# A decode beside a prompt: held time put aside and repaid at a quarter of the running time

## The chip, the core and the metric

The kernel runs on one core of one Trainium2 chip. The metric is the device time of one execution in microseconds. The core has five engines, each with its own queue of instructions that it executes in order: TensorE (PE, matrix products), VectorE (DVE), ScalarE (ACT), GpSimd (POOL) and SyncE (SP, which here only starts transfers). Engines wait for each other by semaphores.

## The reference, cut to what matters

One inference step of a decoder layer for two groups of rows that share the weights: a prompt of 1024 rows, and eight sequences that each add one row ("sample") and attend to 8192 cached rows in pages.

```python
def step(x):                                   # for the prompt and for the sample
    h = rmsnorm(x, g_mix) @ w_in               # q, k, v, forget logit, u, z
    att = fox_attend(q, k, v, cumsum(logf))    # sample: k, v, logf from the paged cache
    sgu = u * (causal_chunk(w_s) @ z + b_s)
    x = x + concat(rmsnorm(att), rmsnorm(sgu)) @ w_o
    x = x + cross_attend(rmsnorm(x), mk, mv, w_cq, w_co)   # 4 heads, 256 memory rows
    x = x + conv_ffn(rmsnorm(x), w_up, conv_w, w_down)     # D_FF = 2816, width 3
    return rmsnorm(x, g_final)

def fox_sample(q, k, v, logf, k_pool, v_pool, logf_pool, page_table):
    k_all = concat(k_pool[page_table], k)
    v_all = concat(v_pool[page_table], v)
    c = cumsum(concat(logf_pool[page_table], logf))
    return fox_attend(q, k_all, v_all, c)      # softmax(q.k / 8 + c_q - c_k) . v
```

All in float32, D_MODEL 1024, 8 attention heads of 64. The outputs also hold the prompt's keys and values, the memory's keys and values (`o_mk`, `o_mv`) and the states for a next step.

## The kernel before

**Arithmetic.** A float32 product is made of three products of rounded parts: `split` writes the high part on ACT (L235, with a scale L238) and the rest on DVE (L236, with a scale L239); `gemm3` (L272 to L274) multiplies high by high, high by low and low by high. Weights come by `wraw` (L249, a 512 KB load that SP starts into one of four buffers `wr`) and are split into `wh` and `wl`.

**The prompt's work** is a Python generator, `prompt()`, which goes through the phases `p1`, `att0`, `attx`, `att1`, and then, for each half of 512 rows, `mid` and `ffn`: `mid0`, `ffn0`, `mid1`, `ffn1`. A `mid` phase is the output projection (`out_proj`, whose products are L1055 to L1057), the norm and transposition (`norm_T`: transposes L1106, splits L239), and cross-attention (`cross`, projections by w_cq and w_co at L1073 to L1075 and in `out_proj`). In cross-attention, for each of four heads: `fetch` loads the head's `o_mk` and `o_mv` (SP, L1126 and L1128); `keys` transposes the keys (PE L1153) and copies them (ACT L1157); `weigh` multiplies queries and keys (PE L1170), takes maxima (DVE L1172), exponentials (ACT L1175, L1178), the reciprocal of the sums (DVE L1181) and scales (ACT L1183); `turned` transposes the weights (PE L1190, copied by ACT L1191); `gather` multiplies by the values (PE L1198) and splits the result, the low part on DVE (L236, `u`). PSUM banks named `ba` and `bb` are used in turn; a bank is free for the next product when the engine that reads it has done so. Each time it has recorded a piece of work, the generator yields `t`, an estimate in microseconds of the TensorE time just recorded.

**The decode** is a second generator, `sample()`: for each sequence 16 K steps and 16 V steps over its cached rows, then `sample_rest()` for the remaining layers of the eight rows. A K step (`kstep`, L1404) fetches 1 MB of keys by an indirect DMA that POOL starts (L1407) into one of four buffers `kv`, multiplies by the query on DVE (L1423) and reduces on DVE (L1427): two multiplies and two reductions in the `mid` phases or while held, one of each of twice the size otherwise. A V step (`vstep`) fetches 1 MB of values (L1469) into the same four buffers and multiplies on PE (L1475, into `dv`; two V steps go to PE together, 16 matmul records in the profile).

**What sets the order.** A loop at the end of `build` takes the prompt's yields one by one. `acc` collects the yielded time; whenever it reaches the pace of the phase (`PACE`, for instance 8.0 us per decode step in `mid0`, 8.5 in `ffn0`, 6.8 in `mid1`, 2.5 in `ffn1`, and 2.9 once the decode has come to its rest), one step of the decode is recorded and the pace taken off. `most` limits how many steps one yield may let through: the whole number of paces in `t`, plus one. `held[0]` stops the decode altogether for a while: `out_proj` sets it after its last group of two row tiles (L1083), `ffn` sets it in its last down-projection when the merge of the second half runs beside it (L1325), and `norm_T` (L1116) and the end of a feed-forward stage (L1888) release it. While it is held, `acc` goes on collecting.

The recorded program then goes through a planner, which re-orders the instructions of each engine by its own costs and due times; DVE and PE instructions of the decode are tied to what was recorded just before them (`behind`, with `last`), so that a step that is recorded later is also planned later.

The lines of the loop that count here:

```python
        acc[0] += t
        most = int(t / PACE[phase[1] or phase[0]]) + 1
        while bgs and not held[0] and most and acc[0] >= PACE[phase[1] or phase[0]]:
            most -= 1
            acc[0] -= PACE[phase[1] or phase[0]]
            w = next(bgs[0], None)
```

Of the kernel before, what the change touches and what calls it, by code (L numbers as in the profile page):

```python
# [78 lines left out]
def build(nc, tc, ctx, a, phases=None):  # L79
# [918 lines left out]
    held = [False]  # L998
# [347 lines left out]
    bgs, acc, phase = [], [0.0], ["p1", None]  # L1346
# [545 lines left out]
    def sample():  # L1892
        yield from decode()
        phase[1] = "rest"
        yield from sample_rest()


    bgs.append(sample())
    seen = 0
    for t in prompt():  # L1900
        ins = nc.cur_bb.bb.instructions
        for e in (ENG.DVE, ENG.PE):
            for i in range(len(ins) - 1, max(seen, len(ins) - 400) - 1, -1):
                if ins[i].engine == e:
                    last[e] = ins[i]
                    break
        if paused[0]:
            t = 0.0
        acc[0] += t
        most = int(t / PACE[phase[1] or phase[0]]) + 1  # L1910
        while bgs and not held[0] and most and acc[0] >= PACE[phase[1] or phase[0]]:
            most -= 1
            acc[0] -= PACE[phase[1] or phase[0]]
            w = next(bgs[0], None)
            if w is None:
                bgs.pop()
            else:
                acc[0] -= (w - 1) * PACE[phase[1] or phase[0]]
        seen = len(nc.cur_bb.bb.instructions)
# [92 lines left out]
```

## Time and profile before

| | us |
|---|---|
| median of 3 runs | 1816.22 (1815.31 to 1817.39) |
| profiled execution | 1820.56 |
| its span | 1818.4 |
| PE busy | 1745.0 (96%) |
| DVE busy | 1397.5 (77%) |
| ACT busy | 734.4 (40%) |
| POOL busy | 510.0 (28%) |

The profile is of one execution, so its own time stands beside its span: 2.16 us lie around the span, and this execution took 4.34 us more than the median. In the rows of the profile, `L1170` is a line of the kernel, `out<-in` names the tiles that an instruction writes and reads, `x8` says how many instructions are grouped, and a bracket such as `[4.19 <-DVE u L236]` gives the idle time of the engine just before them and what ended it. The names of the weights' transfers carry the tile (`wr<-w_co`), those of the decode carry the cache (`kv<-cache_k`). The phases `mid0` to `ffn1` lie at about 560 to 720, 720 to 1110, 1110 to 1360, and from 1360 us to the end of the span.

### The profile page before, as it was taken

How to read it: one execution, taken by the hardware profiler on the slowest of the kernel's cores; microseconds unless marked ns; L12 is line 12 of the kernel's file. 1: busy time of each engine (PE TensorE's matmuls, PEld its weight loads, DVE VectorE, ACT ScalarE, POOL GpSimd, SP SyncE). 2: the span in 40 equal slices, each digit the busy share in tenths (PEclk: the TensorE clock that was granted, in tenths of full speed). 3: DMA queues.
4: the chain of work that ended last, by engine and by line, in shares of the span. 5: the costliest groups of instructions: out<-in, count | busy, mean ns of one | idle time of the engine just before them, and what ended most of it. 6: DMA issues, size and time to landing. Idle time of an engine off the chain costs nothing.

```text
span 1818.4 us, 25090 instructions
## 1 busy us (share of the span) xinstructions
PE 1745.0 (96%) x9637; PEld 1294.9 (71%) x9637; DVE 1397.5 (77%) x1729; ACT 734.4 (40%) x1378; POOL 510.0 (28%) x461
## 2 busy tenths in 40 slices
PE   8999999888998999999999999989899999999997
PEld 5887776656676767777777776766576778767775
DVE  4689668888788877999989899898875549845344
ACT  6332365455643544433333244235353324332332
POOL 1252334332133432223332333334222111011110
PEclk9999999899999999999999999989999999999999
DMA  8886889777696986679878779988787777568982
GB/s 295 306 297 231 302 297 329 242 266 224 219 398 257 342 310 260 257 285 340 316 279 311 271 306 340 381 300 324 290 309 290 267 268 265 179 266 289 359 314 82
DMA packets 157074, 521.06 MB, mean 287 GB/s; under 512 B 20874, under 2 KB 40842, under 8 KB 124186
## 3 DMA queue, kind: packets, MB, share of 16 engines
q0 software_dynamic: 57168, 341.14, 49.5%
q1 hardware_dynamic: 92874, 165.73, 26.4%
q10 hardware_dynamic: 6912, 12.59, 1.8%
q8 instruction: 76, 1.25, 0.3%
q14 instruction: 44, 0.36, 0.1%
HBM read 495.47 MB, written 23.93 MB: 286 GB/s over the span
## 4 chain that ended last, share of the span: by engine, by line
PE 72%; DMA 10%; issue 7%; DVE 6%; ACT 2%; POOL 2%; SPq 0%; POOLq 0%; DVEq 0%; ACTq 0%
PE ba L272 11%; PE ba L274 11%; PE ba L273 11%; PE bb L272 5%; PE bb L273 5%; PE bb L274 5%; PE dv L1475 5%; DMA kv<-cache_k,io 3%; DMA wr<-w_in 2%; DMA kv<-cache_v,io 1%; PE dv L321 1%; PE dv L1751 1%; PE ba L1056 1%; PE ba L1055 1%; PE ba L1057 1%
## 5 line engine op out<-in xcount | busy, mean ns | idle before, releaser
L235 ACT ACTIVATE wh<-wr 128x1024 fp32r<-128x1024 f32 (+2 forms) x220 | 228.9, 1044 | 489.2 <-PE ba L273 156.0
L236 DVE TENSOR_TENSOR wl<-wr,wh 128x1024 fp32r<-128x1024 f32 (+2 forms) x220 | 262.5, 1200 | 175.6 <-PE ba L274 65.7
L1407 POOL DMA_INDIRECT kv<-cache_k,io x128 | 205.6, 1606 | 551.2 <-DVE s L1427 318.9
L1423 DVE TENSOR_TENSOR kv<-kv,d 128x1024 f32<-128x1024 f32 (+1 forms) x156 | 258.0, 1681 | 35.1 <-DMA kv<-cache_k,io 35.1
L1427 DVE TENSOR_REDUCE s<-kv 128x16 f32<-128x1024 f32 (+1 forms) x156 | 258.2, 1674 | 0.1
L1469 POOL DMA_INDIRECT kv<-cache_v,io x128 | 165.3, 1291 | 282.8 <-PE dv L1475 191.8
L272 PE MATMUL ba<-u,wh 128*128 128x512 f32 (+1 forms) x560 | 220.3, 395 | 1.7 <-ACT u L238 1.7
L273 PE MATMUL ba<-u,wh 128*128 128x512 f32 (+1 forms) x560 | 220.2, 393 | 1.7 <-DVE u L239 1.5
L274 PE MATMUL ba<-u,wl 128*128 128x512 f32 (+1 forms) x560 | 219.5, 393 | 0.0
L272 PE MATMUL ba<-wh,u 128*128 128x512 f32 (+1 forms) x495 | 186.9, 379 | 0.9 <-ACT u L235 0.9
L273 PE MATMUL ba<-wl,u 128*128 128x512 f32 (+1 forms) x495 | 185.4, 375 | 1.2 <-DVE wl L236 1.2
L274 PE MATMUL ba<-wh,u 128*128 128x512 f32 (+1 forms) x495 | 183.8, 376 | 0.0
L272 PEld LDWEIGHTS ba<-u,wh 128*128 128x128 f32 x560 | 106.8, 191 | 30.6 <-issue 5.6
L273 PE MATMUL bb<-u,wh 128*128 128x512 f32 (+1 forms) x304 | 119.4, 393 | 9.2 <-DVE u L239 9.2
L274 PEld LDWEIGHTS ba<-u,wl 128*128 128x128 f32 x560 | 106.9, 191 | 29.1 <-issue 6.1
L273 PEld LDWEIGHTS ba<-u,wh 128*128 128x128 f32 x560 | 106.7, 191 | 27.5 <-issue 2.7
L1475 PE MATMUL dv<-kv,s 128*32 128x512 f32 x1024 | 124.2, 598 | 1.8 <-DMA kv<-cache_v,io 1.8
L272 PE MATMUL bb<-u,wh 128*128 128x512 f32 (+1 forms) x304 | 119.4, 393 | 0.0
L274 PE MATMUL bb<-u,wl 128*128 128x512 f32 (+1 forms) x304 | 118.6, 390 | 0.0
L272 PEld LDWEIGHTS ba<-wh,u 128*128 128x128 f32 x495 | 93.0, 188 | 26.0 <-issue 6.9
L274 PEld LDWEIGHTS ba<-wh,u 128*128 128x128 f32 x495 | 92.8, 188 | 21.5 <-issue 3.7
L273 PEld LDWEIGHTS ba<-wl,u 128*128 128x128 f32 x495 | 93.1, 188 | 19.7 <-DVE wl L236 1.9
(425 smaller groups left out, 3255.9 us busy)
## 6 DMA issues: line engine op xcount, KB each, us to landing
wr<-w_up SPq DMA_DIRECT2D x88, 512.0 KB
kv<-w_up POOLq DMA_DIRECT2D x22, 1024.0 KB, 8.0
wr<-w_down SPq DMA_DIRECT2D x40, 512.0 KB
kv<-w_down POOLq DMA_DIRECT2D x11, 1024.0 KB, 8.5
wr<-w_in SPq DMA_DIRECT2D x16, 512.0 KB
wr<-w_o SPq DMA_DIRECT2D x16, 512.0 KB
wr<-w_cq SPq DMA_DIRECT2D x16, 512.0 KB
wr<-w_co SPq DMA_DIRECT2D x16, 512.0 KB
```

The lines of the kernel that those rows point to most:

```text
L235: nc.scalar.activation(h, src, AF.Copy)
L236: nc.vector.tensor_tensor(l, src, h.bitcast(F32), op=ALU.subtract)
L272: mmul(out, sh, mh, start=(i == 0), stop=False)
L273: mmul(out, sh, ml, start=False, stop=False)
L274: mmul(out, sl, mh, start=False, stop=(i == n - 1))
L321: mmul(ps[32 * j : 32 * j + 32, :w], xT[:, k, :] if nk == 8 else xT[:, k * 8 : k * 8 + 32], raw[:, q, j * w : (j + 1) * w], start=(k == 0) ...
L1055: mmul(pss[i], mh[k][:, tb], wh, start=(k == korder[0]), stop=False)
L1407: nc.gpsimd.indirect_dma_start(kv, None, a["cache_k"], off(kidx[:, b, ch : ch + 1]))
L1423: nc.vector.tensor_tensor(kvv[:, i : i + m, :], kvv[:, i : i + m, :], qb.unsqueeze(1).broadcast_to((P, m, 512)), op=ALU.mult)
L1427: nc.vector.tensor_reduce(s[:, ch * 4 + i : ch * 4 + i + m, :].rearrange("p k h -> p (k h)"), kvv[:, i : i + m, :].rearrange("p k (h d) -> ...
L1469: nc.gpsimd.indirect_dma_start(kv, None, a["cache_v"], off(kidx[:, b, ch : ch + 1]))
L1475: mmul(dv[32 * j : 32 * j + 32, :], s[:, ch * 4 : ch * 4 + 4, :].rearrange("p k h -> p (k h)"), kvv[:, j, :], start=(ch == 1), stop=(ch == ...
```

## The change

Time that is yielded while the decode is held goes into a second account, `late`, and not into `acc`. At each yield outside a held spell a quarter of the yield's own time, as long as `late` holds that much, is moved from `late` to `acc`, in addition to the time itself. `most` is still worked out from `t` alone.

```diff
     bgs.append(sample())
-    seen = 0
+    seen, late = 0, 0.0
     for t in prompt():
...
         if paused[0]:
             t = 0.0
-        acc[0] += t
+        if held[0]:
+            late += t
+        else:
+            more = min(late, t / 4)
+            late -= more
+            acc[0] += t + more
         most = int(t / PACE[phase[1] or phase[0]]) + 1
         while bgs and not held[0] and most and acc[0] >= PACE[phase[1] or phase[0]]:
```

## The prediction

> **What bounds the kernel.** I read the page first (busy shares, chain), then the waits of TensorE (PE), then the 20-us windows around the five places where the decode is held, then the timelines of PE, DVE, ACT, POOL and SP at the waits found there.
>
> ```profile
> span 1818.4 us, 25090 instructions
> PE 1745.0 (96%) x9637; PEld 1294.9 (71%) x9637; DVE 1397.5 (77%) x1729; ACT 734.4 (40%) x1378; POOL 510.0 (28%) x461
> PE 72%; DMA 10%; issue 7%; DVE 6%; ACT 2%; POOL 2%; SPq 0%; POOLq 0%; DVEq 0%; ACTq 0%
> ```
>
> PE is busy 96% of the span and holds 72% of the chain that ended last. The 73.4 us in which it is not busy are all that an order can win, and whatever adds to them moves the end one for one wherever PE is dense behind it. The profiled execution took 1820.56 us, 2.16 us beside its span and 4.34 us over the median of 1816.22 us; I work out differences on the profile and add them to the median.
>
> ```profile
> PE bb L273 <- DVE u L239: 9.2, 5, 5.6
> PE bb L1170 <- DVE u L236: 4.2, 1, 4.2
> PE ba L1170 <- ACT t L1157: 2.6, 3, 1.6
> PE dv L1475 <- DMA kv<-cache_v,io: 1.8, 2, 1.7
> ```
>
> These are PE's waits (total us, times, longest) that belong to places where the changed rule acts. The longest two, 5.6 and 4.2 us, are waits for DVE, whose K steps (L1423, L1427) stand in the same queue. Other long waits (for w_in, for L808) lie in phases that the change doesn't reach.
>
> ```profile
> 620.00:640.00 20.00, 18.77 (x93) 12.64 (x92) 19.89 (x23) 14.81 (x40) 7.67 (x5) 1.00 1.01 375
> 720.00:740.00 20.00, 20.00 (x105) 14.98 (x104) 14.45 (x17) 9.40 (x17) 3.71 (x3) 1.00 0.40 148
> 740.00:760.00 20.00, 20.00 (x96) 14.78 (x95) 20.00 (x21) 6.40 (x11) 6.28 (x5) 1.00 0.85 320
> 1180.00:1200.00 20.00, 13.96 (x81) 11.20 (x80) 18.07 (x28) 9.49 (x20) 6.82 (x5) 0.74 0.80 285
> 1260.00:1280.00 20.00, 13.87 (x64) 8.87 (x62) 15.19 (x18) 12.29 (x33) 9.05 (x4) 0.96 0.94 345
> 1380.00:1400.00 20.00, 20.00 (x105) 13.33 (x107) 10.45 (x15) 7.28 (x13) 4.56 (x5) 1.00 0.93 340
> ```
>
> The columns are the window, its length, busy time (and instructions) of PE, weight loads, DVE, ACT and POOL, then PE's granted clock, the DMA share and GB/s. The starts of the two feed-forward stages (720 to 760, 1380 to 1400) leave PE no idle time; the cross-attention stages do (13.96 and 13.87 of 20), with DVE at 15 to 20.
>
> **The change, part by part.** No instruction is added or removed. While `held[0]` stands, the prompt's time goes to `late` and not to `acc`; afterwards each yield adds a quarter of its own `t` from `late`. By the code there are five held spells, of 13 to 15.7 us. Before, a spell's time stood in `acc` at its end and `most` let one decode step through at nearly every yield until it was spent; now steps come at 1.25 times the pace and the debt is paid over some 50 to 65 us of prompt time. Following `acc` through both versions, both record the same 290 decode steps; only one step, at most two, is recorded later at any yield, in four stretches: A, the cross-attention of the first half (about 10 yields); B, the start of the first feed-forward stage (9); C, the second half from its start to the output projection of its cross-attention (43); D, the start of the second feed-forward stage (until the debt is paid). The planner then orders each engine's instructions anew. In its order the 64 pairs of V steps on PE (16 matmuls each) mostly move by 0 to 15 prompt matmuls, two in C by 21; on POOL and SP a handful of DMA issues trade places, none is added.
>
> *B and D: 0.* PE is at 20.00 of 20 us there, and a V pair that moves by 15 matmuls only trades places with work PE does anyway. What covers it is that density. Without it, later pairs would free their `kv` buffers later and the next fetches on POOL would slip; I bound that at −0.5 to +2 us (the upper end is one pair's wait for its V data, 1.7 us in the waits above) and take 0.
>
> *A: +1.4 us.*
>
> ```profile
> 623.68 1.92 PE L1475 MATMUL dv<-kv,s 128*32 128x512 f32 x16 [0.18 <-DMA kv<-cache_v,io]
> 625.53 1.99 PE L1170 MATMUL bb<-t,u 128*128 128x256 f32 x8
> 633.03 0.63 PE L1153 MATMUL ba<-cp,t 128*128 128x128 f32 x4 [0.34 <-DMA t<-o_mk]
> 635.45 3.72 PE L1170 MATMUL ba<-t,u 128*128 128x256 f32 x16 [0.68 <-ACT t L1157]
> 623.66 0.59 ACT L1157 ACTIVATE t<-bb 128x512 f32<-128x512 f32 x1
> 630.44 1.69 ACT L1183 ACTIVATE u<-u,cr 128x256 f32<-128x256 f32 x4
> ```
>
> Rows give start and duration in us and in brackets the wait ahead. The keys that L1170 multiplies are copied by ACT at L1157, 623.66 to 624.25, while PE does a V pair. In the new order that pair stands behind the eight L1170, and on ACT the four L1183 (1.69 us, at 630.44 before) stand ahead of L1157. PE comes to L1170 at 623.5 and waits until 624.25 + 1.69 = 625.9: +2.4 us. Of that the waits of 0.34 and 0.68 us that followed are absorbed: 2.4 − 1.0 = +1.4. The lower bound is −1.0 (L1183 done early, as one K step fewer stands ahead of the reciprocal on DVE, and both small waits gone).
>
> ```profile
> 622.87 0.37 SPq L249 DMA_DIRECT2D wr<-w_co  x1
> 623.33 0.42 SPq L1126 DMA_DIRECT2D t<-o_mk  x1
> 625.10 3.76 SPq L249 DMA_DIRECT2D wr<-w_co  x3
> ```
>
> For the upper bound: SP's queue now has three w_co loads ahead of the o_mk load, where it had one. Two of the three that took SP 3.76 us go ahead, so o_mk is issued about 2.5 us later, and 1 MB more shares the DMA queues at 375 GB/s (2.8 us). L1153 waits for o_mk, and was 0.34 us late already. Of 5.3 us the 2.4 us above cover part: up to +3 more, so A reaches from −1.0 to +4.4. I take no price for it, since fewer K and V fetches are in flight there.
>
> *C, the norm ahead of cross-attention: +0.2 us.*
>
> ```profile
> 1193.97 0.58 PE L273 MATMUL bb<-u,wh 128*128 128x256 f32 x1 [5.59 <-DVE u L239]
> 1190.05 1.21 DVE L1427 TENSOR_REDUCE s<-kv 128x16 f32<-128x1024 f32 x1
> 1191.18 2.35 DVE L1423 TENSOR_TENSOR kv<-kv,d 128x1024 f32<-128x1024 f32 x2
> 1193.44 0.47 DVE L239 SCALAR_TENSOR_TENSOR u<-ba,gp,u 128x256 fp32r<-128x256 f32 x1
> ```
>
> PE waits 5.59 us for one split (L239), which stands on DVE behind two reductions and two multiplies of K steps. If the change thinned this burst, the wait would go. In the new order it doesn't: between the first splits and the awaited one stand again two reductions and two multiplies, with small moves among them; +0.2 for a small scalar operation moved ahead. Bounds: one reduction less or more, −1.2 and +1.2.
>
> *C, the gather: +4.3 us.* This term carries the forecast.
>
> ```profile
> 1278.40 3.64 PE L1170 MATMUL bb<-t,u 128*128 128x256 f32 x8 [4.19 <-DVE u L236]
> 1288.92 1.12 PE L1198 MATMUL ba<-u,t 128*128 128x512 f32 x2 [0.58 <-ACT u L1191]
> 1261.66 6.22 POOL L1407 DMA_INDIRECT kv<-cache_k,io  x1 [5.18 <-DVE s L1427]
> DMA to landing us min/median/max: 5.5/8.7/13.7
> 1259.04 1.22 DVE L236 TENSOR_TENSOR wl<-wr,wh 128x1024 fp32r<-128x1024 f32 x1
> 1260.17 1.21 DVE L1427 TENSOR_REDUCE s<-kv 128x16 f32<-128x1024 f32 x1
> 1264.70 2.35 DVE L1423 TENSOR_TENSOR kv<-kv,d 128x1024 f32<-128x1024 f32 x2
> 1267.06 0.66 DVE L1172 TENSOR_REDUCE cmx<-ba 128x2 f32<-128x512 f32 x1
> 1267.64 2.33 DVE L1427 TENSOR_REDUCE s<-kv 128x16 f32<-128x1024 f32 x2
> 1269.89 0.68 DVE L1172 TENSOR_REDUCE cmx<-ba 128x2 f32<-128x512 f32 x1
> 1275.38 2.36 DVE L1423 TENSOR_TENSOR kv<-kv,d 128x1024 f32<-128x1024 f32 x2 [4.81 <-DMA kv<-cache_k,io]
> 1277.66 0.69 DVE L236 TENSOR_TENSOR u<-bb,u 128x512 fp32r<-128x512 f32 x1
> ```
>
> The fourth line is the time from issue to landing of transfers into `kv` between 1200 and 1300 us. L1170 needs the bank `bb`, which DVE frees at 1277.66 with `u` (L236); that stood behind a K multiply that waited 4.81 us for a K fetch issued on POOL at 1261.66 and landed 13.7 us later, the slowest of the window. So in the old order only one multiply lies between the late landing and `u`; both maxima (L1172) and the first K step's reductions were done while DVE waited. In the new order both K steps' multiplies come first, then reduction, maximum, reduction, maximum, two reductions, then `u`. Everything behind the second multiply waits for K. The reduction that frees the buffer stands one L236 earlier (1.1 us), so the fetch is issued near 1260.5. Landing 13.7 us on: 1274.2 + 2.36 + 4 × 1.17 + 2 × 0.67 = 1282.6, and `u` is done at 1283.3 where it was done at 1278.35: +4.9. The 0.58 us at 1288.92 is absorbed: +4.3. With the median of 8.7 us: landing 1269.2, `u` done 1278.3: 0. With 5.5 us K is there before the first multiply ends at 1267.05: `u` done 1276.2, −2.2. I take 13.7, the row of this very fetch, whose POOL time of 6.22 us recurs if its surroundings do; the ends are −2.2 and +4.9.
>
> A rule weighed against a row. After the wait of 4.19 us the eight L1170 took 3.64 us, against 1.99 us for the same eight at 625.53: a wait of this length costs 1.65 us more than itself. The Trainium skill, "TensorE: Matmul & The Clock Gate", Part 1, says that the array's clock halves after an idle window of about 3.4 us and comes back after as long a busy one; the two rows agree with it. By that rule the gather costs the same 1.65 before and after in my sum, and a wait shortened below it would give the 1.65 back.
>
> Sum: 1.4 + 0.2 + 4.3 + 0 = +5.9, so 1816.2 + 5.9 = 1822 us.
>
> **Rivals.**
> *No change.* The K fetch lands near its median (gather 0), A's wait is mostly absorbed (+1): 1817 us. For it: no work is added, PE is at 20.00 of 20 us in B and D, and the fetch's 6.22 us on POOL may be chance. Against: the new DVE order holds more work behind that fetch.
>
> *Faster.* The K fetch at the gather lands within about 7 us, before the first multiply ends. Then PE's wait there falls from 4.19 to 2.0 us, the slow eight L1170 give 1.65 back, and A gains 1.0: −2.2 − 1.65 − 1.0 = −4.9, 1811 us. It decides from a landing under 8.7 us. For it: minimum 5.5, and POOL's fetches stand further apart. Against: the DMA share is 0.94 in that window.
>
> *Larger slowdown.* The o_mk load behind three w_co loads costs +3 in A on top. PE's wait at one place there would then pass 3.4 us; by the measured 1.65 us that is +4.7 altogether: 1822 + 4.7 = 1827 us. For it: it was 0.34 us late already, DMA share 1.01. Against: one K fetch fewer there. (The skill's clock rule, above, is what would make that 4.7 rather than 3.)
>
> **How the numbers follow.** About 3.6 us, 0.2%, is what can be told from no change. Forecast 0.44 (1820 to 1825), larger slowdown 0.12, no change 0.26, faster 0.18. Slower: 0.44 + 0.12 = 0.56 less a little for a forecast that falls just inside 3.6 us: 0.55; same 0.26; faster 0.19. The upper end is the larger slowdown with C's bounds (1.2 + 0.6): 1829; the lower end is the faster case, 1811.
>
> **What would show it.** Right: PE's wait for `u` L236 at the gather near 9 us instead of 4.2; a wait of about 2 us for `t` L1157 near 624; the wait for L239 still at 5 to 6; B and D at 20.00. Wrong: the gather's wait gone or under 3 us, the K fetch there taking under 9 us, or new waits in B, C or D that the old order hid, among them one for o_mk.

## The result and the profile after

The changed kernel takes 1819.85 us in the median (20 runs, 1813.76 to 1827.23), the kernel before 1815.83 (20 runs, 1805.25 to 1819.11): a ratio of 1.0026, 95% interval 1.0015 to 1.0037, or +4.7 us (+2.7 to +6.7). The forecast was slower, by 5.9 us, at 1822.

The profiled execution after took 1817.95 us with a span of 1816.2, shorter than the profiled execution before (1818.4). So the two profiles cannot simply be subtracted: executions of the changed kernel differ by 13 us among themselves, and each profile is one of them. What the two show is where the waits moved. PE's waits after (total us, times, longest):

```profile
span 1816.2 us, 25099 instructions
PE 1743.6 (96%) x9637; PEld 1294.3 (71%) x9637; DVE 1397.8 (77%) x1729; ACT 732.9 (40%) x1378; POOL 494.7 (27%) x461
PE bb L273 <- DVE u L239: 11.6, 5, 5.7
PE dv L1475 <- DMA kv<-cache_v,io: 4.7, 3, 3.0
PE ba L1190 <- ACT u L1178: 2.5, 1, 2.5
PE bb L1170 <- ACT t L1157: 1.5, 1, 1.5
```

The busy times are almost the same (POOL's is 15 us less); the wait of 4.2 us for `u` L236 is gone, the wait for the splits (L239) has grown from 9.2 to 11.6 us, there is a new wait for the exponentials L1178, the predicted wait for `t` L1157, and V pairs now wait 4.7 us for their values where it was 1.8. The 20-us windows at these places after (columns as in the prediction):

```profile
720.00:740.00 20.00, 20.00 (x102) 15.23 (x101) 14.06 (x14) 8.69 (x13) 3.75 (x3) 1.00 0.43 141
900.00:920.00 20.00, 16.96 (x76) 11.36 (x75) 16.13 (x18) 4.14 (x7) 5.12 (x4) 0.91 0.89 341
1180.00:1200.00 20.00, 12.26 (x72) 9.44 (x65) 16.00 (x23) 7.78 (x17) 3.87 (x4) 0.84 0.66 231
1260.00:1280.00 20.00, 16.38 (x79) 11.18 (x78) 17.15 (x19) 12.61 (x35) 6.48 (x5) 0.91 0.95 371
```

The start of the first feed-forward stage is as dense as before, but at 900 us the same stage has lost 3 us; before, that window was full:

```profile
900.00:920.00 20.00, 20.00 (x96) 14.80 (x95) 17.63 (x20) 6.05 (x9) 5.78 (x5) 1.00 0.87 326
```

The norm of the second half has lost 1.7 (12.26 against 13.96), and the gather has gained 2.5 (16.38 against 13.87).

### The profile page after: what moved, and what is told of

Read it like the earlier page. It is cut to its first block, busy times and chain, and to the rows that moved or that the text cites. A ratio compares the mean times of both kernels' runs of the same rounds, so it can differ in the third digit from the quotient of the medians.

```text
span 1816.2 us, 25099 instructions
## 1 busy us (share of the span) xinstructions
PE 1743.6 (96%) x9637; PEld 1294.3 (71%) x9637; DVE 1397.8 (77%) x1729; ACT 732.9 (40%) x1378; POOL 494.7 (27%) x461
## 4 chain that ended last, share of the span: by engine, by line
PE 54%; issue 11%; DVE 7%; DMA 4%; POOL 3%; ACT 3%; DVEq 0%; POOLq 0%; ACTq 0%; SPq 0%
PE ba L272 7%; PE ba L274 7%; PE ba L273 7%; PE dv L1475 4%; PE bb L272 3%; PE bb L274 3%; PE bb L273 3%; DMA kv<-cache_v,io 3%; POOL kv L1407 2%; PE dv L321 1%; DVE kv L1423 1%; PE dv L1751 1%; PE bb L843 1%; DVE s L1427 1%; PE ba L1057 1%
## 5 line engine op out<-in xcount | busy, mean ns | idle before, releaser
L236 DVE TENSOR_TENSOR wl<-wr,wh 128x1024 fp32r<-128x1024 f32 (+2 forms) x220 | 261.9, 1198 | 175.6 <-PE ba L274 56.7
L1407 POOL DMA_INDIRECT kv<-cache_k,io x128 | 196.4, 1534 | 582.8 <-DVE s L1427 320.4
L1469 POOL DMA_INDIRECT kv<-cache_v,io x128 | 157.5, 1230 | 263.9 <-PE dv L1475 193.0
L273 PE MATMUL bb<-u,wh 128*128 128x512 f32 (+1 forms) x304 | 118.3, 389 | 11.6 <-DVE u L239 11.6
```

Of the source, the lines that this page charges most:

```text
L236: nc.vector.tensor_tensor(l, src, h.bitcast(F32), op=ALU.subtract)
L273: mmul(out, sh, ml, start=False, stop=False)
L1407: nc.gpsimd.indirect_dma_start(kv, None, a["cache_k"], off(kidx[:, b, ch : ch + 1]))
L1469: nc.gpsimd.indirect_dma_start(kv, None, a["cache_v"], off(kidx[:, b, ch : ch + 1]))
```

## The experiments

All kernels are compared with the kernel before on the same chip. `only_x` applies the new rule to some of the five held spells and adds the time of the others to `acc` as before:

```diff
+        if held[0] and not stood:
+            spell += 1
+        stood = held[0]
-        if held[0]:
+        if held[0] and spell in (...):
             late += t
+        elif held[0]:
+            acc[0] += t
         else:
```

The sets are (1,) for only_a, (2,) for only_b, (3, 4) for only_c and (5,) for only_d; (1, 3, 4, 5) for no_b and (1, 2, 5) for no_c.

> Only the first held spell (first half, output projection to the norm ahead of cross-attention) is put aside and repaid at a quarter; every other held time goes to acc as before. Only the order of the first cross-attention (570 to 700 us) should differ from the kernel before. The prediction's working: +1.4 us, with a wait of about 2 us for t L1157 near 622. The rival drawn from the one profile after (A took 66.15 us there against 66.24, from the first L1153 to the second output projection): 0 us, the wait of 1.5 us paid back by smaller waits behind it.

> Only the second held spell (output projection of the first cross-attention to the norm ahead of the first feed-forward stage) is put aside. The prediction's working: 0 us, PE dense at 20.00 of 20. The rival from the profile after: a V pair in the first feed-forward stage waits 3 us for its values because a K fetch ahead of it held POOL for 4.8 us; if that belongs to the order and not to chance, this kernel is 4 to 7 us slower and the wait of dv L1475 near 907 us returns.

> Only the third and fourth held spells (end of the first feed-forward stage; output projection of the second half) are put aside: the second half's norm and cross-attention get the new order. The prediction's working: +4.5 us (+0.2 at the norm, +4.3 at the gather). The rival from the profile after: +3 at the norm (two waits for L239, 2.0 and 5.7 us) and a gain of up to 5 at the gather if POOL's fetch there takes 1.7 us and not 6.2; together -2 us.

> Only the fifth held spell (output projection of the second cross-attention to the norm ahead of the second feed-forward stage) is put aside. Both theories: 0 us within 1 us, PE at 20.00 of 20 from 1360 us on. Its first 1300 us have the order of the kernel before, so its profile is also a second look at the gather of the old order: the prediction says that the K fetch there takes about 6 us on POOL again and PE waits 4 us; the rival says that the 6.2 us was one draw of several.

| kernel | ratio to before | 95% interval | in us |
|---|---|---|---|
| changed | 1.0026 | 1.0015 to 1.0037 | +4.7 |
| only_a | 0.9989 | 0.9978 to 1.0001 | −2.0 |
| only_b | 1.0029 | 1.0015 to 1.0042 | +5.3 |
| only_c | 1.0023 | 1.0008 to 1.0038 | +4.2 |
| only_d | 1.0004 | 0.9991 to 1.0017 | +0.7 |

B alone makes a slowdown as large as the whole change's, though the prediction gave it 0; C alone makes +4.2 where 4.5 were forecast; D shows no change. The parts add to 8.2 us and the whole is 4.7; with intervals of 2 us or more to either side of each, that does not show whether they are independent.

Since each profile is one execution, I measured stages in all of them. The times below are worked out from the starts of rows: the first cross-attention from its first L1153 to the next L1055; the first feed-forward stage from the end of the norm's L1106 to the next L1055; the second half from that L1055 to the L1055 of its second output projection.

| profile | first cross-attention | first feed-forward stage | second half |
|---|---|---|---|
| before | 66.2 | 415.2 | 160.2 |
| only_d | 65.9 | 413.9 | 158.5 |
| only_a | 65.9 (new) | 413.8 | 156.0 |
| only_b | 65.0 | 419.0 (new) | 158.5 |
| only_c | 65.7 | 413.3 | 155.9 (new) |
| changed | 66.2 (new) | 419.2 (new) | 157.8 (new) |

"New" marks the stretch whose spell was put aside; the planner also shifted the order of the second half in only_a and only_b, so that there only only_d repeats the old one.

The feed-forward column is sharp: 413.3 to 415.2 in the old order, 419.0 and 419.2 in the new. B's cost was nowhere near its start. PE and POOL of the changed kernel:

```profile
888.98 4.76 POOL L1407 DMA_INDIRECT kv<-cache_k,io  x1 [9.20 <-PE dv L1475]
894.05 0.94 POOL L1469 DMA_INDIRECT kv<-cache_v,io  x1 [0.30 <-issue]
895.29 0.94 POOL L1469 DMA_INDIRECT kv<-cache_v,io  x1 [0.31 <-issue]
```

```profile
907.27 3.31 PE L1475 MATMUL dv<-kv,s 128*32 128x512 f32 x16 [3.04 <-DMA kv<-cache_v,io]
910.51 0.50 PE L274 MATMUL ba<-wh,u 128*128 128x512 f32 x1
```

Before, the same rows are

```profile
888.89 1.58 POOL L1407 DMA_INDIRECT kv<-cache_k,io  x1 [9.53 <-PE dv L1475]
890.78 2.55 POOL L1469 DMA_INDIRECT kv<-cache_v,io  x1 [0.30 <-issue]
893.63 1.94 POOL L1469 DMA_INDIRECT kv<-cache_v,io  x1 [0.30 <-issue]
905.91 1.92 PE L1475 MATMUL dv<-kv,s 128*32 128x512 f32 x16
```

Now the K fetch holds POOL for 4.76 us, the two V fetches go out behind it, and the pair that needs them waits 3.04 us and then runs 16 matmuls in 3.31 us instead of 1.92. All four profiles with B in the new order have the 4.76 us; the pair's wait in them is 1.57 us (only_b, where the 16 matmuls took 1.92 us as before), 2.00, 3.04 and 3.15.

Why 4.76? DVE in the same stretch of the changed kernel:

```profile
888.92 2.27 DVE L1423 TENSOR_TENSOR kv<-kv,d 128x2048 f32<-128x2048 f32 x1
891.12 1.21 DVE L236 TENSOR_TENSOR wl<-wr,wh 128x1024 fp32r<-128x1024 f32 x1
892.25 0.67 DVE L1293 TENSOR_TENSOR t<-t,t 128x512 f32<-128x512 f32 x1
892.86 0.73 DVE L1286 SCALAR_TENSOR_TENSOR t<-bb,gp,t 128x511 f32<-128x511 f32 x1
```

The fetch started at 888.98, within a run of three DVE operations that read two operands from SBUF; the run ended at 892.92, and the fetch at 893.74, 0.82 us later. That is a pattern: in the profiles of the kernel before, the changed kernel and the first four experiments, the 854 fetches that start outside such runs take 0.94 us in the median, and 2.7 at most but for two of 4.54 us that start 0.3 us ahead of a run. Of the 730 that start within one, 528 end 0.7 to 0.95 us after the run's end. For 405 of these, only the operation then running was left. Where more of the run was still to come (310 fetches), 123 waited for all of it, up to 6.3 us, and 177 ended as long after the end of an earlier operation: they slipped in between two operations of the run. The Trainium skill, "SBUF — State Buffer", "Who interferes with whom", says that a VectorE instruction with two SBUF inputs contends with a GpSimd instruction that reads SBUF, and that of two that contend the one that comes second is blocked until the first is done. The rows agree with this, and differ from that section's inference that `tensor_tensor` leaves the issue of a DMA alone; a run without a gap can also block as one.

The hold on POOL is only a part of the pair's wait. The time from start to landing of the two V fetches can be read in the kernel before and in after_look, the changed kernel's second profile (the views of L1469, 890 to 896 us and 895 to 898 us):

```profile
DMA to landing us min/median/max: 7.1/7.8/8.6
DMA to landing us min/median/max: 10.2/11.1/12.0
```

Counted from the start of the stage, the V pair that frees the K fetch's buffer ends 3.5 us later in after_look, so the fetch starts 3.5 us later; the second V fetch starts 5.1 us later and takes 12.0 us to land instead of 8.6; the pair that needs it comes to PE 1.7 us later. The longer hold thus adds 1.6 us at most to a landing that is 8.6 us later in all. The buffers freed later and the slower transfers make the rest.

The other column that mattered was not settled by these four: only_c is slower by 4.2 us, but its profiled execution, one of the shortest of that kernel (1813.9 of a median of 1818.9), has a second half of 155.9 us. So I took second profiles, and tested the runs of DVE operations by breaking them up.

> The changed kernel once more, for a second profile: its times spread from 1813.8 to 1827.2 us, the kernel before's by half of that. Theory of the prediction: where the execution is slow (over 1818 us), the fetch of K ahead of the gather lands late and PE waits there for 5 us or more. Rival: the slow executions lose their time in the first feed-forward stage, where a V pair waits for its values after a K fetch that held POOL for 4.8 us.

> The kernel with the third and fourth spell put aside once more: its first profile was of a fast execution (1813.9 us of a median of 1818.9), in which the gather was 5 us shorter than in the old order and the norm 3.5 us longer. Theory of the prediction: in a slow execution the stretch from the norm to the last output projection (86.8 us in the first profile) is 5 us or more longer, and the waits stand behind late K or V data. Rival: the norm alone (44.3 us against 40.3) makes the difference, and the rest is spread over the span.

These two repeat the changed kernel and only_c without an edit. after_look took 1821.28 us, only_c_look 1816.43. The first feed-forward stage is 420.2 us in after_look, with the same wait again,

```profile
908.55 3.64 PE L1475 MATMUL dv<-kv,s 128*32 128x512 f32 x16 [3.15 <-DMA kv<-cache_v,io]
```

and 415.2 in only_c_look; the second halves are 159.2 and 158.7. Neither shows a late K fetch at the gather. The rival of the first expectation holds as far as B goes. only_c's +4.2 us shows in neither of its profiles, whose second halves of 155.9 and 158.7 us stand against 160.2 and 158.5 in the old order; C was still open.

after_il and only_a_il make every K step of the changed kernel and of only_a out of halves, and tie the second multiply behind the first reduction:

```diff
-            sp = KS if phase[0][:3] == "mid" or held[0] else 1
+            sp = KS
...
                 for i in range(0, 4, m):
+                    with tc.issue_after(nc.cur_bb.bb.instructions[-1]) if i else nullcontext():
-                    nc.vector.tensor_tensor(
+                        nc.vector.tensor_tensor(
...
-                for i in range(0, 4, m):
                     nc.vector.tensor_reduce(
```

> The changed kernel with every K step in halves, multiply, reduction, multiply, reduction (before: both multiplies, then both reductions, or one of each of twice the size), so that runs of two-input DVE operations get shorter. If POOL's fetches wait for such runs (they end 0.81 us after the run in all profiles so far, up to 6.3 us in all) and their lateness makes the time, the fetches of over 4 us become rarer, and the time falls by 3 to 6 us. If the time is made by the order around the norm and the splits alone, nothing changes; DVE work grows by some 4 us, off the path.

> The kernel with only the first spell put aside (0.9989 of the time before), with the K steps in halves as well. If shorter runs help there too, 1808 to 1811 us, which would beat both kernels; if not, 1812 us.

after_il: 1.0039 of the kernel before (1.0024 to 1.0053), only_a_il: 1.0024 (1.0009 to 1.0038). Fetches of over 4 us fell from 8 to 1 in the profile, and the pair in the first feed-forward stage no longer waits 3 us. Yet the stage took 420.8 us, with other waits at its end, and against the changed kernel's profile this one lost 7 us before the second output projection and 7 us behind the second half, while the second half shrank to 150.3 us. So the late fetches went with the long runs, as the first theory said, but the time did not fall by the 3 to 6 us that it expected: breaking the runs everywhere also gave the kernel another order, with waits at other places.

The last four undo one part, or change the one size in the rule.

> All held spells put aside but the second. If the slowdown is that of the first feed-forward stage (419.0 to 420.2 us in three profiles with the second spell put aside, 413.3 to 415.3 in five without), this kernel has the time of the one before: 1814 to 1816 us. The prediction's working (+1.4 in A, +4.5 in C) says 1820 to 1822 us.

> All held spells put aside but the third and fourth. If the first feed-forward stage makes the slowdown, 1818 to 1821 us, as the changed kernel; by the prediction's working (nothing in B, all in C) 1816 to 1818 us.

no_b: 1.0014 (1.0001 to 1.0028), +2.5 us; no_c: 1.0034 (1.0018 to 1.0051), +6.2 us. Taking B out halves the slowdown by these figures, though the interval overlaps the changed kernel's, and its median of 1819.25 us lies in neither expected range; its profile has a first feed-forward stage of 414.2 us against 417.1 in no_c. Taking C out does not help: no_c, at 1822.07 us, is above both expected ranges. And no_b's profiled execution, 1823.59 us, is the one that shows what C costs when it does cost. PE, POOL and DVE of no_b at the gather:

```profile
1279.17 1.12 PE L1190 MATMUL ba<-cp,u 128*128 128x128 f32 x4 [9.59 <-ACT u L1178]
```

```profile
1258.69 5.09 POOL L1407 DMA_INDIRECT kv<-cache_k,io  x1 [2.90 <-DVE s L1427]
```

```profile
1258.33 4.62 DVE L236 TENSOR_TENSOR wl<-wr,wh 128x1024 fp32r<-128x1024 f32 x4
1262.87 0.17 DVE L1181 RECIPROCAL cr<-cl 128x4 f32<-128x4 f32 x1
1262.96 2.33 DVE L1423 TENSOR_TENSOR kv<-kv,d 128x1024 f32<-128x1024 f32 x2
1272.45 2.36 DVE L1423 TENSOR_TENSOR kv<-kv,d 128x1024 f32<-128x1024 f32 x2 [7.16 <-DMA kv<-cache_k,io]
1274.72 1.22 DVE L1427 TENSOR_REDUCE s<-kv 128x16 f32<-128x1024 f32 x1
1275.85 0.68 DVE L1172 TENSOR_REDUCE cmx<-ba 128x2 f32<-128x512 f32 x1
1280.42 0.69 DVE L236 TENSOR_TENSOR u<-bb,u 128x512 fp32r<-128x512 f32 x1
```

The K fetch started 0.36 us into a run of four L236, ended 0.83 us behind it, and landed at 1272.4, 13.8 us after it started. DVE waited 7.16 us, and reductions, maxima and `u` all lay behind: PE stood still for 9.59 us. This is the chain that the prediction described, in its order and nearly in its sizes (5.09 us on POOL where 6.22 were assumed, 13.8 us to landing where 13.7 were); PE waits at L1190 and not at L1170, because the exponentials of the maxima that are late too come first in its queue. In the changed kernel's own profile the same fetch, in the same place, ended 0.82 us after the first of the four:

```profile
1260.73 1.68 POOL L1407 DMA_INDIRECT kv<-cache_k,io  x1 [4.04 <-DVE s L1427]
1260.38 4.62 DVE L236 TENSOR_TENSOR wl<-wr,wh 128x1024 fp32r<-128x1024 f32 x4
1268.74 2.36 DVE L1423 TENSOR_TENSOR kv<-kv,d 128x1024 f32<-128x1024 f32 x2 [1.37 <-DMA kv<-cache_k,io]
1275.46 1.11 PE L1190 MATMUL ba<-cp,u 128*128 128x128 f32 x4 [2.48 <-ACT u L1178]
```

From about 1210 us to the second output projection, the order of instructions on PE, DVE, ACT and POOL is the same in the two profiles. So one order has two outcomes: 1.68 us on POOL and a wait of 2.5 to 3.6 us on PE (four profiles, second halves of 155.9 to 159.2 us), or 5.09 us and a wait of 9.59 (one profile, 164.7 us). The difference, 164.7 less the mean of 157.9, is 6.8 us. no_b's twelve times fall into six from 1814.0 to 1817.6 and six from 1820.9 to 1827.4, whose means are 6.8 us apart. That fits but shows little: no_c, which has the old rule for C, splits into halves 7.8 us apart, and only one profile has been seen on the long side.

> Repaid at half of the running time instead of a quarter, all spells. If paying back more slowly costs in proportion, about half of the slowdown: 1818 us. If it is the chance position of single fetches and V pairs in the new order, the time can lie on either side, 1812 to 1821 us, and the first feed-forward stage has other waits than the 3 us for values near 190 us from its start.

> Repaid at an eighth of the running time. In proportion to how long the debt stands: slower than with a quarter, 1822 to 1826 us. If chance positions decide: anywhere within 1812 to 1824 us, with waits for values at other places of the first feed-forward stage.

These change `t / 4` to `t / 2` and to `t / 8`. half: 0.9965 (0.9951 to 0.9980), −6.4 us, faster than both kernels at 1809.54 us and below both expectations; eighth: 1.0039 (1.0025 to 1.0053). The time does not go in proportion: against the kernel before, half, a quarter and an eighth stand at −6.4, +4.7 and +7.1 us. In half's profile the first feed-forward stage takes 414.3 us, as in the old order, although B is put aside there too; the second half takes 150.9 us, and PE's time in the norm is

```profile
1180.00:1200.00 20.00, 16.29 (x100) 11.74 (x99) 19.71 (x32) 9.34 (x22) 5.18 (x5) 0.91 0.94 351
1191.64 0.39 PE L273 MATMUL bb<-u,wh 128*128 128x256 f32 x1 [1.23 <-DVE u L239]
1187.58 2.36 DVE L1423 TENSOR_TENSOR kv<-kv,d 128x1024 f32<-128x1024 f32 x2
1190.72 1.26 DVE L239 SCALAR_TENSOR_TENSOR u<-ba,gp,u 128x256 fp32r<-128x256 f32 x3
1191.89 2.33 DVE L1427 TENSOR_REDUCE s<-kv 128x16 f32<-128x1024 f32 x2
PE bb L273 <- DVE u L239: 5.8, 6, 2.1
```

where three awaited splits at once stand ahead of the K step's reductions: PE's waits of `bb` for a split add up to 5.8 us in the whole kernel, the longest 2.1, against 9.2 and 5.6 before. No DVE operation at its gather waits for K. eighth has a gather without a late K as well, but loses 4 us in the first feed-forward stage (418.4), where a V pair waits 2.2 us at another place, and 7 us behind the second half.

## Why the prediction was right, and where it was not

- **Bound and method.** PE at 96% with few waits, and one to one behind them: right. No instruction was added (the engines' counts are the same). In the first feed-forward stage the lost time is in waits and in the slower matmuls behind them, as the rows show; for the whole kernel no pair of profiles shows it.
- **Profile against median.** The working took the profile before as typical but for an offset of 4.3 us. The stretch from the norm's first transpose (L1106) to the next L640 in the first half took 28.92 us there, and 26.9 to 27.0 in ten of eleven later profiles (those with K steps in halves left out), so 2 us of that offset may lie in one place.
- **A, +1.4.** The wait for `t` L1157 came as told (1.45 to 1.73 us in five profiles, 2.4 forecast), with the four L1183 ahead of it. It was paid back almost whole: 66.25 us in the mean of five profiles with A against 65.7 in five without, +0.5. In none of these five did PE wait for o_mk there. That only_a took 2.0 us less than before (interval −4.0 to +0.2) is not from A's stretch; its second half has another order and took 156.0 us, against 159.3 in the mean of before and only_d.
- **B, 0: the step that failed.** "PE is at 20.00 of 20 us there, and a V pair that moves by 15 matmuls only trades places with work PE does anyway." It holds at the start of the stage (20.00 from 720 to 740 us after, too). But the steps recorded late there moved the planner's order through the whole stage, not for nine yields: four profiles with B give 417.1 to 420.2 us (mean 418.9), six without it 413.3 to 415.2 (414.3): +4.6, and +5.3 by the times of only_b. Of the 4.6, by PE's rows, 3.0 are idle time and 1.6 slower matmuls. The mechanism was named in the prediction: without the density, later pairs free their buffers later and the next fetches slip. That is what happened some 170 us into the stage, where the K fetch also met a run of two-input DVE operations. What failed is the term: density at the stage's start was taken to cover it, at 0, and its bound of +2 was one wait of 1.7 us. The wait was 1.6 to 3.2 us, up to 1.7 us of slower matmuls stood behind it, and at the stage's end stands another wait of 1.43 us. half has that last wait and not the first, and its stage is no longer than the old one, which points to the wait for values as the larger part. In only_b the matmuls behind the 1.43 us took 0.63 us instead of 0.39, in the other three they did not:

```profile
1112.19 0.79 PE L272 MATMUL bb<-wh,u 128*128 128x512 f32 x1 [1.43 <-ACT u L235]
1112.79 0.63 PE L273 MATMUL bb<-wl,u 128*128 128x512 f32 x1
```

In no_c the same rows are

```profile
1113.25 0.50 PE L272 MATMUL bb<-wh,u 128*128 128x512 f32 x1 [1.43 <-ACT u L235]
1113.59 0.39 PE L273 MATMUL bb<-wl,u 128*128 128x512 f32 x1
```

- **C, the norm, +0.2.** The wait for the split stayed at 5.5 to 5.7 us, as told, but a second one of 2.0 us came ahead of it (0.44 before). DVE is not later there: in all seven of these profiles, PE starts behind that wait 4.9 to 5.2 us after the end of the projection (L1073). But the V pair that ran on PE in between, 0.7 us after the projection's end, now runs 5.6 to 5.8 us ahead of that end and no longer covers the wait. The prediction let pairs trade places at no cost. From the first L1073 of the second half to the end of the norm: 43.9 us in five profiles with C, 40.3 in two with the old order, less 1.85 for a further V pair that lies in this stretch now: +1.7.
- **C, the gather, +4.3.** Right as a mechanism, wrong in taking it as one value. From the end of the norm to the second output projection, with the same V pair added: 98.2 us in no_b's profile with the long fetch, against 94.0 in the two of the old order, +4.2; 91.0 in the mean of four with the short fetch, −3.0. The prediction took the fetch's 6.22 us as what "recurs if its surroundings do". In the old order it did (6.23 in only_d), in the new one a long fetch came in one profile of five. By these profiles C comes to −1.3 us with the short fetch and +5.9 with the long one; only_c measured +4.2, so its times must hold something that its two profiles do not show, and where that lies stays open.
- **Sum.** By the profiles 0.5 + 4.6 + 1.7 and −3.0 or +4.2 at the gather: 3.8 or 11.0 us. The measured +4.7 with a spread up to 1827 us lies near the first, and both profiles of the changed kernel have the short fetch. So the direction and nearly the size came out with B's 4.6 us in the place of the gather's 4.3. That is luck: by the prediction's own signs, the profile after shows those of being wrong (the gather's wait for `u` gone, its K fetch landed within 9 us, a new wait in B). How often the changed kernel's fetch is the long one stays open.
- **Rivals.** The faster one was half true: the gather's fetch is short in four profiles of five, and the gather gains 3 us then. It was outweighed by B and the norm, which it left out. The larger slowdown by o_mk in A did not come.
- **Clock.** The prediction weighed a rule of the Trainium skill, "TensorE: Matmul & The Clock Gate", Part 1, that the clock halves after an idle window of about 3.4 us, against two rows, and both agreed. Other rows show that the length of one wait does not settle it. The V pair took 3.31 and 2.94 us instead of 1.92 behind waits of 3.04 and 2.00 us. The wait of 1.43 us above was followed by a granted clock of 0.50 over 3.4 us in only_b and of 1.00 in no_c, half and the changed kernel. At the gather a wait of 2.51 us was followed by eight L1170 in 1.99 us in only_c, one of 2.48 us by eight in 3.08 us in the changed kernel. So the 1.65 us need not have been saved by a wait just below that window, nor lost by one above it.

## What to carry to other kernels

When a change only re-times what a planner sees, follow the planned order to the end of the stage and beyond, not only to where the recording agrees again: density on the bounding engine hides moved work, not moved transfers. A transfer whose issue can be blocked has two arrival times; price what stands behind it at both, and look at more than one profile. And try the size in the rule: here a repayment at half took 6.4 us off where a quarter added 4.7.

## What the runs showed of the hardware

An indirect fetch on POOL that starts within an unbroken run of two-input DVE operations may end only some 0.81 us after the whole run, so that it takes up to 6.3 us instead of 0.94, or may slip in between two of them: the same order of instructions in the same place took 1.68 us in four profiles and 5.09 in one. The same wait of PE can be followed by full or by half clock: 1.43 us at one place by a granted clock of 0.50 in only_b and of 1.00 in no_c, half and the changed kernel. Either can make executions differ at a place; whether they make the whole spread of the times is not shown. Before, it was 14 us over 20 runs, for the changed kernel 13, for no_c 18 over 12 runs.
